# Slots turned by the expert's number, one expert's transposes queued later, and a rearranged last sequence

## The chip, the cores and the metric

The kernel runs on one core of one Trainium2 chip. The metric is the device time of one execution in microseconds (us). Before the change three runs gave 1287.1, 1283.97 and 1284.54 us; the median is 1284.54 us.

## The reference, cut to what matters

One layer of a hybrid decoder over 512 tokens of 1024 channels in float32: a mixer (an mLSTM head group beside causal pooling), then a mixture of experts, then a last RMSNorm.

```
x   = x + concat([ym, yp]) @ W_out
h   = RMSNorm(x)
logits = h @ w_router + b_router                    # 512 x 32
top_vals, top_idx = top_k(logits, 4)                # four experts a token
gates = softmax(top_vals)
for every expert e, for the tokens that chose it:
    gate = min(h @ w_gate[e] + b_gate[e], 7)        # 1024 x 1024
    up   = clip(h @ w_up[e] + b_up[e], -7, 7)       # 1024 x 1024
    y    = (gate * sigmoid(1.702 * gate) * (up + 1)) @ w_down[e] + b_down[e]
    x[token] += gates[token, e] * y
out = RMSNorm(x)
```

Each of the 32 experts has three weight matrices of 4 MB, so the experts' weights alone are 12 MB an expert and 403 MB (384 MiB) in all. With the reference's inputs an expert gets between 30 and 113 of the 2048 token choices.

## The kernel before

The mixer and the router take the first part of the span; from about 228 us on the kernel works through the experts. A table made in the program sets their order: experts 0 and 1 come first, and the last one has few tokens (30), so that only its blocks 0 and 1 are used and its blocks 2 and 3 are skipped by branches.

**Weights.** The SP queue streams all weights into a ring of slots of 2 MB each (128 partitions by 4 x 1024 floats; `load_chunks`, L114 to L147: w_gate and w_up by L141 as halves of 1 MB, w_down by L144 as whole slots). A load is issued as soon as its slot is free, that is, when TensorE has read the weights that lay there. The slots' names in the trace are wr, ym, wlo and whi.

**Slots of the tokens.** The router ranks each token choice among those of its expert (`place`). The rank divided by 32 is the block, and the rank modulo 32 is the slot (L710, `sfk`). A block is a tile of 128 partitions by 256 floats: token slot s with quarter q of its 1024 channels sits on partition 32q + s. POOL gathers the blocks from the table h2d by row indices (L931, 1 KB a row) and adds the results into the table yd (L1121; blocks 0 and 1 together as a pair with 2 KB a row, blocks 2 and 3 with 1 KB). Slots without a token have an index out of bounds and move no row. These transfers go through the queue that the page calls software_dynamic, beside SP's weights on the same 16 DMA engines.

**Start of the experts.** `xpose(e)` (L959) turns the gathered blocks by four VectorE transposes into the left operands xt. `softmax` (L1093 to L1097) makes the gates, `gates_rows(t)` (L1103 and L1106, VectorE) makes the rows of 128 tokens that `gates_product(t)` (L1114, TensorE) turns into gates by slot. The four products stand between the four quarters of expert 0's w_gate and w_up matmuls (`each`, L1001), so TensorE can't go on with the next quarter before the product's rows are there.

**The last sequence.** After the last expert but one the order of TensorE, VectorE, ACT and POOL is written out by hand: the string FIN (L39). A letter is a step, a digit a block or a group of 128 tokens. D and E are the first and second half of the last w_down matmuls of a block (L1069). Steps s, r and f are for the tokens not in the last expert, read back from yd by SP (L1177): the sum of squares (s, L1180 ACT), the scale (r, L1184 VectorE and L1185 POOL), and the scaling with the store to the output (f, L1188 VectorE and L1209 SP). Steps a, q, n, m and p are for the last expert's blocks: the add and its squares (a, L1214 VectorE, L1215 ACT), the sum over the four quarters (q, L1218 TensorE), the norm (n, L1222 VectorE, L1223 POOL), the multiplication (m, L1227 VectorE) and the scatter of the finished rows into the output (p, L1200 POOL, which writes over rows that the stores of f have written and so waits for all four of these).

Of the kernel before, what the change touches and what calls it, by code (L numbers as in the profile page):

```python
# [12 lines left out]
I32 = mybir.dt.int32  # L13
U32 = mybir.dt.uint32
AF = mybir.ActivationFunctionType
OP = mybir.AluOpType
# [4 lines left out]
S, D = 512, 1024  # L21
# [5 lines left out]
EPS = 1e-5  # L27
LIMIT = 7.0
ALPHA = 1.702
NB = 4  # L30
# [5 lines left out]
LN = 0  # L36

FIRST = 2
FIN = "D2 D3 D0 D1 s0 r0 s1 r1 f0 s2 r2 f1 s3 r3 f2 E2 E3 a2 a3 q2 q3 f3 n2 n3 m2 p2 m3 p3 E0 E1 a0 q0 a1 q1 n0 n1 m0 p0 m1 p1"  # L39
ENDM = ("PE", "DVE", "Activation", "Pool")  # L40
HA = (False, False)
DBG = {}
# [131 lines left out]
def mixer(tc, nc, ctx, g):  # L174
    pe, act, dve, gp, sp = nc.tensor, nc.scalar, nc.vector, nc.gpsimd, nc.sync
# [75 lines left out]
    n1 = tc.tile_pool(name="n1", bufs=1)  # L251
# [119 lines left out]
    for hpart in (hhi, hlo):  # L371
        for k in range(NK):
            pe.matmul(ps[:100], wg[:, k, :], hpart[:, k, :], start=(hpart is hhi and k == 0),
                      stop=(hpart is hlo and k == NK - 1))
# [4 lines left out]
    r, m = (at.tile([128, S], F32, name=n, tag="mb", bufs=2)[0:H] for n in "rm")  # L379
# [228 lines left out]
    def early():  # L608
# [5 lines left out]
    v8, ebk, sfk, gi, cnt, iota_e, iota_eb, tok4, qbig = (  # L614
        g[k] for k in ("v8", "ebk", "sfk", "gi", "cnt", "iota_e", "iota_eb", "tok4", "qbig"))
# [86 lines left out]
    def place(t):  # L702

        o = R[t]
        dve.tensor_tensor(o["oh"], o["oh"], o["rank"][:, None, :].to_broadcast([128, 4, NE]), op=OP.mult)
        rk, bi = (rp.tile([128, 4], I32, name=n, tag=n, bufs=2) for n in ("rk", "bi"))
        with nc.allow_low_precision("ranks are whole numbers under 512"):
            dve.tensor_reduce(rk, o["oh"], axis=AX.X, op=OP.add)
        dve.tensor_scalar(bi, rk, 5, None, op0=OP.arith_shift_right)
        dve.tensor_scalar(sfk[:, t, :], rk, 31, None, op0=OP.bitwise_and)  # L710
        dve.scalar_tensor_tensor(ebk[:, t, :], o["xf"], 16.0, bi, op0=OP.mult, op1=OP.add)
        o["s"] = rp.tile([128, 4, 32], F16, name="ohs", tag="ohs", bufs=2)
        o["e"] = rp.tile([128, 4, 128], F16, name="rh", tag="rh", bufs=1)
        dve.tensor_tensor(o["s"], iota_e[:, None, :].to_broadcast([128, 4, 32]),
                          sfk[:, t, :, None].to_broadcast([128, 4, 32]), op=OP.is_equal)
# [183 lines left out]
def moe(tc, nc, ctx, g):  # L899
    pe, act, dve, gp, sp = nc.tensor, nc.scalar, nc.vector, nc.gpsimd, nc.sync  # L900
    const, ident = (g[k] for k in ("const", "ident"))
    gi, gs, cnt, h2d, yd, sfk, ebk, gates_k, v8, iota_e, iota_eb = (
        g[k] for k in ("gi", "gs", "cnt", "h2d", "yd", "sfk", "ebk", "gates_k", "v8", "iota_e", "iota_eb"))
    W, load_chunks, rstd_of, nhalf, out = (g[k] for k in ("W", "load_chunks", "rstd_of", "nhalf", "out"))
# [3 lines left out]
    with tc.tile_pool(name="mo", bufs=1) as mo, tc.tile_pool(name="mop", bufs=1, space=PSUM) as pp:  # L908
# [5 lines left out]
        yb = pp.tile([128, 512], F32, name="yb")  # L914
# [37 lines left out]
        def xpose(e):  # L952
            XT[e] = []
            for b in range(NB):
                if e == 0 and b == 2:
                    for ps in gub[2:] + [dbq]:
                        dve.memset(ps, 0.0)
                t = mo.tile([128, 256], F32, name=f"xt{b}", tag=f"xt{b}", bufs=2) if b < 3 else xgt[:, 4]
                i = dve.transpose(t, xg[b])  # L959
                if b:  # L960
                    tc.keep_in_program_order(i)
                XT[e].append(t)
# [136 lines left out]
        def gates_rows(t):  # L1099

            o = mo.tile([128, 4, 32], F32, name="o32", tag="t", bufs=4)
            r = mo.tile([128, 4, 128], F32, name="r32", tag="t", bufs=4)
            dve.tensor_tensor(o, iota_e[:, None, :].to_broadcast([128, 4, 32]),  # L1103
                              sfk[:, t, :, None].to_broadcast([128, 4, 32]), op=OP.is_equal)
            for k in range(4):
                dve.tensor_scalar(r[:, k, :], iota_eb, ebk[:, t, k:k + 1], gates_k[:, t, k:k + 1],  # L1106
                                  op0=OP.is_equal, op1=OP.mult)
            ROWS[t] = o, r

        def gates_product(t):  # L1110
            o, r = ROWS[t]
            for k in range(4):
                for q in range(4):
                    pe.matmul(yb[q * 32:(q + 1) * 32, :128], o[:, k, :], r[:, k, :], start=(t == 0 and k == 0),  # L1114
                              stop=(t == NT - 1 and k == 3))
            if t == NT - 1:
                dve.tensor_copy(gs, yb[:, :128])
                pairs()
# [60 lines left out]
        def square(a, junk, sums, t):  # L1179
            act.activation(junk, a[:, t], AF.Square, accum_out=sums[:, 2 * t:2 * t + 1])  # L1180
# [6 lines left out]
        def result(a, nfb, t):  # L1187
            dve.scalar_tensor_tensor(a[:, t], a[:, t], RS[t], nfb, op0=OP.mult, op1=OP.mult)  # L1188
# [5 lines left out]
        def finish(a, nfb, yg, nfq, junk, quarters, sums):  # L1194

            e = NE - 1
            orows = out[0].rearrange("t (q n) -> (t q) n", q=4)

            def put(b):
                i = gp.indirect_dma_start(out=orows, out_offset=bass.IndirectOffsetOnAxis(  # L1200
                    ap=gi[:, e * NB + b:e * NB + b + 1], axis=0), in_=zs[b], in_offset=None,
                    bounds_check=S * 4 - 1, oob_is_err=False)
                for o in puts.values():
                    tc.declare_no_dep(i.ins, o.ins, reason="an expert's tokens differ")
                puts[b] = i

            def store(t):
                result(a, nfb, t)
                sp.dma_start(out[0, t * 128:(t + 1) * 128, :], a[:, t])  # L1209

            zs = [yg[:, b * 256:(b + 1) * 256] for b in range(NB)]

            def add(b):
                dve.scalar_tensor_tensor(zs[b], db[b], gs[:, e * NB + b:e * NB + b + 1], zs[b], op0=OP.mult, op1=OP.add)  # L1214
                act.activation(junk[:, :256], zs[b], AF.Square, accum_out=sums[:, 2 * b:2 * b + 1])  # L1215

            def sumq(b):
                pe.matmul(yb[:, b:b + 1], quarters, sums[:, 2 * b:2 * b + 1], start=True, stop=True)  # L1218

            def norm(b):  # L1220
                r = sums[:, 2 * b + 1:2 * b + 2]
                dve.tensor_scalar(r, yb[:, b:b + 1], 1.0 / D, EPS, op0=OP.mult, op1=OP.add)  # L1222
                gp.tensor_tensor(r, r, nhalf[:, 0:1], op=OP.pow)  # L1223

            def mul(b):
                r = sums[:, 2 * b + 1:2 * b + 2]
                dve.scalar_tensor_tensor(zs[b], zs[b], r, nfq, op0=OP.mult, op1=OP.mult)  # L1227

            def final_put(b):
                with tc.If(GR[e] > 32 * b) if b > 1 else ExitStack():  # L1230
                    put(b)

            todo = dict(s=lambda t: square(a, junk, sums[:, 8:], t), r=lambda t: scale(sums[:, 8:], t), f=store, a=add, q=sumq, n=norm, m=mul, p=final_put,
                        d=lambda b: some(e, d_mm, b, range(8)), D=lambda b: some(e, d_mm, b, range(4)),
                        E=lambda b: some(e, d_mm, b, range(4, 8)))
            for step in FIN.split():
                todo[step[0]](int(step[1]))
# [7 lines left out]
        xpose(0)  # L1245
        softmax()
        gates_rows(0)
        gates_rows(1)
        g["order"].close()
        order = ExitStack()  # L1250
        order.enter_context(tc.manual_schedule(engines={mybir.EngineType.PE}))
# [1 line left out]
        for kind, e in g["way"]:  # L1253
            if kind == "gu":
                with tc.issue_after(last[0]):
                    CR[e] = pe.value_load(tokens(e), min_val=0, max_val=S)
                if e + 1 < NE:
                    gather(e + 1)
                    xpose(e + 1)
                if e:  # L1260
                    bias(0, gb, 0, 512)
                    act.activation(gbs, gb, AF.Copy)
                if e + 1 < NE:
                    select(e + 1, 0)
                each(e, gu_mm)
                load_chunks(4)
                if e == NE - 1:
                    select(e, 1)
                act_blocks(e)
                continue  # L1270
            if e < NE - 1:
                select(e, 1)
                halves(e)
                each(e, d_mm)
            load_chunks(2)
            if e < NE - 1:
                scatter_all(e)
            if e == NE - 2:
                final = finish_early()
                order.close()  # L1280
                end = ctx.enter_context(ExitStack())
                end.enter_context(tc.manual_schedule(engines={getattr(mybir.EngineType, n) for n in ENDM}))
# [137 lines left out]
```

## Time and profile before

| | |
|---|---|
| median of three runs | 1284.54 us |
| the profiled execution's own time | 1286.53 us |
| its span | 1284.8 us |
| TensorE busy | 1160.3 us (90%) |
| VectorE busy | 496.6 us (39%) |
| moved by DMA | 454.54 MB, mean 354 GB/s |
| of it software_dynamic (gathers, scatters) | 17.59 MB in 11264 packets |
| granted TensorE clock, mean | 0.968 |

The span is the profiled time from the first instruction to the last; the execution's own time is 1.7 us longer. The DMA share of a stretch is the mean busy share of the core's 16 DMA engines: about 1 means that all of them are busy, and a lower value means that some or all are idle. In the rows of a timeline the bracket tells how long the engine sat idle before the instruction and what ended that.

### The profile page before, as it was taken

The numbers are of one execution on the slowest core, as the hardware profiler recorded it, in microseconds if no ns is written. First come the engines' busy times: TensorE is split into PE (matmuls) and PEld (weight loads), VectorE is DVE, ScalarE is ACT, GpSimd is POOL, SyncE is SP. The second block draws the span as 40 slices with busy tenths as digits, with TensorE's granted clock in tenths as the row PEclk, the third lists the DMA queues.
The fourth block names the chain that finished last, engine by engine and source line by source line (L and its number), as shares of the span: only waits on it lengthen the run. The fifth ranks groups of instructions, "written<-read, shape, count | busy, mean of one in ns | idle before, by whom it ended". The sixth has DMA issues, their size and how long they took to land. (4 is left out here: it accounts for less than half of the span.)

```text
span 1284.8 us, 24782 instructions
## 1 busy us (share of the span) xinstructions
PE 1160.3 (90%) x9818; PEld 497.6 (39%) x9819; DVE 496.6 (39%) x1263; ACT 274.2 (21%) x592; POOL 212.8 (17%) x259
## 2 busy tenths in 40 slices
PE   8999999789887899999989998889979999989973
PEld 5787676323232233333323333233323333334321
DVE  4684756354432422234333342333332232233433
ACT  4593453102111101012111111111101011111212
POOL 3011021102211101121111211012201111111022
PEclk9999999989998999999989999889999999999997
DMA  9731766779999999999999999999999999999972
GB/s 325 253 112 33 235 228 235 265 294 405 408 412 414 419 415 387 413 390 413 407 412 406 412 404 402 414 408 404 407 404 405 406 406 404 402 400 408 411 291 83
DMA packets 81800, 454.54 MB, mean 354 GB/s; under 512 B 12766, under 2 KB 27222, under 8 KB 40283
## 3 DMA queue, kind: packets, MB, share of 16 engines
q1 hardware_dynamic: 67674, 428.58, 82.6%
q0 software_dynamic: 11264, 17.59, 5.6%
q10 hardware_dynamic: 2688, 5.90, 1.3%
q8 instruction: 129, 2.11, 0.7%
q14 instruction: 45, 0.36, 0.1%
HBM read 439.69 MB, written 16.92 MB: 355 GB/s over the span
## 5 line engine op out<-in xcount | busy, mean ns | idle before, releaser
L1001 PE MATMUL gub<-wr,xt 128*32 128x512 f32 x3520 | 409.6, 616 | 48.2 <-PEq L979 15.3
L1011 DVE TENSOR_TENSOR t<-gub,gbs 128x512 f32<-128x512 f32 x128 | 85.4, 686 | 565.9 <-PE gub L1001 340.8
L1001 PEld LDWEIGHTS gub<-wr,xt 128*32 128x32 f32 x3520 | 131.7, 113 | 308.5 <-issue 294.8
L931 POOL DMA_INDIRECT xgt<-h2d,gi x81 | 83.5, 1031 | 728.2 <-DVE t L1012 511.4
L949 ACT ACTIVATE par<-ident 128x128 fp32r<-128x128 f32 x64 | 19.4, 305 | 448.0 <-PEq L981 214.7
L1014 ACT ACTIVATE sg<-t 128x256 f32<-128x256 f32 x128 | 52.4, 413 | 250.9 <-DVE t L1012 250.9
L1389 DVE TENSOR_TENSOR sg<-sg,t 128x256 f32<-128x256 f32 x128 | 52.4, 423 | 87.4 <-ACT sg L1014 87.2
L1055 PE MATMUL dbp<-wr,at 128*32 128x512 f32 x736 | 84.1, 604 | 0.0
L1055 PE MATMUL yb<-wr,at 128*32 128x512 f32 x672 | 76.4, 594 | 0.1
L1001 PE MATMUL gub<-whi,xt 128*32 128x512 f32 x512 | 60.4, 607 | 6.0 <-DMA whi<-in_w_up_dram 6.0
L1121 POOL DMA_INDIRECT yd<-yp,gip x31 | 50.3, 1623 | 92.0 <-ACT yp L1133 87.2
L1001 PE MATMUL gub<-wlo,xt 128*32 128x512 f32 x512 | 58.8, 594 | 6.8 <-DMA wlo<-in_w_up_dram 3.1
L1001 PE MATMUL gub<-ym,xt 128*32 128x512 f32 x512 | 61.2, 607 | 3.0 <-DMA ym<-in_w_up_dram 3.0
L1021 DVE STREAM_TRANSPOSE at<-sg 128x256 f32<-128x256 f32 x96 | 60.9, 635 | 0.1
L1390 DVE SCALAR_TENSOR_TENSOR sg<-t,sg 128x256 f32<-128x256 f32 x128 | 49.8, 409 | 0.1
L240 DVE TENSOR_TENSOR wlo<-wraw,whi 128x1024 fp32r<-128x1024 f32 x30 | 36.7, 1223 | 28.7 <-ACT whi L239 28.6
L959 DVE STREAM_TRANSPOSE xt<-xgt 128x256 f32<-128x256 f32 x96 | 40.8, 426 | 6.0 <-DMA xgt<-h2d,gi 6.0
L1055 PEld LDWEIGHTS dbp<-wr,at 128*32 128x32 f32 x736 | 23.3, 111 | 50.5 <-issue 47.5
L1069 PE MATMUL dbq<-wr,at 128*32 128x256 f32 x672 | 39.6, 384 | 0.8 <-DMA wr<-in_w_down_dram 0.8
L239 ACT ACTIVATE whi<-wraw 128x1024 fp32r<-128x1024 f32 x30 | 31.7, 1059 | 40.0 <-PE sc L294 11.0
L1055 PEld LDWEIGHTS yb<-wr,at 128*32 128x32 f32 x672 | 21.7, 110 | 45.6 <-issue 43.9
L1015 DVE TENSOR_SCALAR t<-t 128x256 f32<-128x256 f32 x128 | 36.4, 284 | 0.0
(366 smaller groups left out, 1318.1 us busy)
## 6 DMA issues: line engine op xcount, KB each, us to landing
wr<-in_w_down_dram SPq DMA_DIRECT2D x45, 2048.0 KB
wr<-in_w_gate_dram SPq DMA_DIRECT2D x89, 1024.0 KB
wr<-in_w_up_dram SPq DMA_DIRECT2D x89, 1024.0 KB
ym<-in_w_gate_dram SPq DMA_DIRECT2D x13, 1024.0 KB
ym<-in_w_up_dram SPq DMA_DIRECT2D x13, 1024.0 KB
wlo<-in_w_gate_dram SPq DMA_DIRECT2D x13, 1024.0 KB
wlo<-in_w_up_dram SPq DMA_DIRECT2D x13, 1024.0 KB
whi<-in_w_gate_dram SPq DMA_DIRECT2D x13, 1024.0 KB
```

Source lines behind the costliest of these rows:

```text
L240: low.tensor_tensor(l3, rv, h3.bitcast(F32), op=OP.subtract)
L931: return gp.indirect_dma_start(out=xg[b], out_offset=None, in_=h2d, in_offset=bass.IndirectOffsetOnAxis(ap=(gi0 if e < FIRST else gi)[:, e ...
L959: i = dve.transpose(t, xg[b])
L1001: i = pe.matmul(gub[b][q * 32:(q + 1) * 32, :], XT[e][b][:, c * 32:(c + 1) * 32], w[:, :, c % 2, q * 256:(q + 1) * 256], start=(c == 0), s ...
L1011: dve.tensor_tensor(t, gub[b], gbs, op=OP.add)
L1014: act.activation(sg, t[:, 0:256], AF.Sigmoid, scale=ALPHA)
L1021: dve.transpose(AT[e, b].rearrange("p (c s) -> p c s", c=8), sgs[b].rearrange("p (i c) -> p c i", c=8))
L1055: i = pe.matmul(dbp[r:r + 32, :], AT[e, b][:, c * 32:(c + 1) * 32], w[:, c % 4, h * 512:(h + 1) * 512], start=False, stop=(c == 7))
L1069: i = pe.matmul(quarter(e, b)[q * 32:(q + 1) * 32, :], AT[e, b][:, c * 32:(c + 1) * 32], w[:, c % 4, q * 256:(q + 1) * 256], start=False, ...
L1121: i = gp.indirect_dma_start(out=to, out_offset=bass.IndirectOffsetOnAxis(ap=index, axis=0), in_=y, in_offset=None, bounds_check=rows - 1, ...
L1389: dve.tensor_tensor(sg, sg, t[:, 0:256], op=OP.mult)
L1390: dve.scalar_tensor_tensor(sg, t[:, 256:], 1.0, sg, op0=OP.add, op1=OP.mult)
```

## The change

Three things are changed.

First, the slot of a token choice is no longer its rank modulo 32 but that number turned by exclusive-or with the number of its expert (L710, one VectorE instruction for one). The block stays the same. For an expert whose tokens fill no whole block, the rows that are missing were always those of the highest slots; now they lie elsewhere for each expert.

Second, the transposes of expert 1 may be issued on VectorE only behind the last instruction of `gates_rows(1)`.

Third, FIN is reordered: E of all blocks comes ahead of the adds, the four adds stand together ahead of f2 and f3, and one norm over the four blocks takes the place of four. The scatters of blocks 2 and 3, which are branched around here, come last.

```diff
-FIN = "D2 D3 D0 D1 s0 r0 s1 r1 f0 s2 r2 f1 s3 r3 f2 E2 E3 a2 a3 q2 q3 f3 n2 n3 m2 p2 m3 p3 E0 E1 a0 q0 a1 q1 n0 n1 m0 p0 m1 p1"
+FIN = "D2 D3 D0 D1 s0 r0 s1 r1 f0 s2 r2 f1 s3 r3 E2 E3 E0 E1 a2 a3 a0 a1 f2 q2 q3 q0 q1 f3 n0 m0 p0 m1 p1 m2 p2 m3 p3"
...
-        dve.tensor_scalar(sfk[:, t, :], rk, 31, None, op0=OP.bitwise_and)
+
+        dve.scalar_tensor_tensor(sfk[:, t, :], rk, 31, o["xf"].bitcast(I32), op0=OP.bitwise_and, op1=OP.bitwise_xor)
...
-                dve.tensor_scalar(r[:, k, :], iota_eb, ebk[:, t, k:k + 1], gates_k[:, t, k:k + 1],
-                                  op0=OP.is_equal, op1=OP.mult)
+                i = dve.tensor_scalar(r[:, k, :], iota_eb, ebk[:, t, k:k + 1], gates_k[:, t, k:k + 1],
+                                      op0=OP.is_equal, op1=OP.mult)
             ROWS[t] = o, r
+            return i
...
-            def norm(b):
-                r = sums[:, 2 * b + 1:2 * b + 2]
-                dve.tensor_scalar(r, yb[:, b:b + 1], 1.0 / D, EPS, op0=OP.mult, op1=OP.add)
-                gp.tensor_tensor(r, r, nhalf[:, 0:1], op=OP.pow)
+            rq = sums[:, NB:2 * NB]
+
+            def norm(_):
+                dve.tensor_scalar(rq, yb[:, 0:NB], 1.0 / D, EPS, op0=OP.mult, op1=OP.add)
+                gp.tensor_tensor(rq, rq, nhalf, op=OP.pow)
...
-        gates_rows(1)
+        rows_made = gates_rows(1)
...
-                    xpose(e + 1)
+                    with ExitStack() if e else tc.issue_after(rows_made.ins):
+                        xpose(e + 1)
```

Where a line number of the changed kernel is meant, it is one higher than before from L711 on, two or three higher from the end of `gates_rows` on.

VectorE at the start of the experts, before. The first row is softmax's, the four transposes (xt_2152 to xgt) are expert 1's, gip is the index table of the pairs, o and r are the rows of the gates:

```order
L1093 TENSOR_SCALAR nv<-v_68 128x4
L959 STREAM_TRANSPOSE xt_2152<-xgt 128x256
L941 UNCONDITIONAL_BRANCH
L959 STREAM_TRANSPOSE xt_2154<-xgt 128x256
L959 STREAM_TRANSPOSE xt_2156<-xgt 128x256
L959 STREAM_TRANSPOSE xgt<-xgt 128x256
L1084 TENSOR_SCALAR gip<-gi 32x32 x2
L971 UNCONDITIONAL_BRANCH
L941 UNCONDITIONAL_BRANCH
L1084 TENSOR_SCALAR gip<-gi 32x32 x2
L1096 RECIPROCAL nv<-nv 128x4
L1097 TENSOR_TENSOR gates_k<-gates_k,nv 128x16
```

Behind these rows stand the rows of gates_rows(0) and gates_rows(1).

The same place in the changed kernel:

```order
L1094 TENSOR_SCALAR nv<-v_68 128x4
L1085 TENSOR_SCALAR gip<-gi 32x32
L942 UNCONDITIONAL_BRANCH
L1085 TENSOR_SCALAR gip<-gi 32x32 x3
L1097 RECIPROCAL nv<-nv 128x4
L1098 TENSOR_TENSOR gates_k<-gates_k,nv 128x16
L1104 TENSOR_TENSOR o_2103<-iota_e,sfk 128x128
L1107 TENSOR_SCALAR r_2104<-iota_eb,ebk,gates_k 128x128 x4
L1104 TENSOR_TENSOR o_2110<-iota_e,sfk 128x128
L1107 TENSOR_SCALAR r_2111<-iota_eb,ebk,gates_k 128x128 x4
L960 STREAM_TRANSPOSE xt_2152<-xgt 128x256
L960 STREAM_TRANSPOSE xt_2154<-xgt 128x256
```

The gates and the rows of the first two products now stand ahead of expert 1's transposes; nothing else changes places with them.

VectorE in the last sequence, before, from r3 on. wr_13381 holds the token groups, wr_13382 the last expert's blocks and the sums; gub_2041, gub_2042, dbp and dbq are the matmul results of blocks 2, 3, 0 and 1:

```order
L1184 TENSOR_SCALAR wr_13382<-wr_13382 128x1
L1188 SCALAR_TENSOR_TENSOR wr_13381<-wr_13381,wr_13382 128x1024
L1214 SCALAR_TENSOR_TENSOR wr_13382<-gub_2041,gs,wr_13382 128x256
L1214 SCALAR_TENSOR_TENSOR wr_13382<-gub_2042,gs,wr_13382 128x256
L1188 SCALAR_TENSOR_TENSOR wr_13381<-wr_13381,wr_13382 128x1024
L1222 TENSOR_SCALAR wr_13382<-yb 128x1 x2
L1227 SCALAR_TENSOR_TENSOR wr_13382<-wr_13382 128x256 x2
L1214 SCALAR_TENSOR_TENSOR wr_13382<-dbp,gs,wr_13382 128x256
L1230 UNCONDITIONAL_BRANCH x2
L1214 SCALAR_TENSOR_TENSOR wr_13382<-dbq,gs,wr_13382 128x256
L1222 TENSOR_SCALAR wr_13382<-yb 128x1 x2
L1227 SCALAR_TENSOR_TENSOR wr_13382<-wr_13382 128x256 x2
```

These are f2, a2, a3, f3, then norm and multiplication of blocks 2 and 3, and last the same steps for blocks 0 and 1.

And in the changed kernel:

```order
L1186 TENSOR_SCALAR wr_13382<-wr_13382 128x1
L1216 SCALAR_TENSOR_TENSOR wr_13382<-gub_2041,gs,wr_13382 128x256
L1216 SCALAR_TENSOR_TENSOR wr_13382<-gub_2042,gs,wr_13382 128x256
L1216 SCALAR_TENSOR_TENSOR wr_13382<-dbp,gs,wr_13382 128x256
L1216 SCALAR_TENSOR_TENSOR wr_13382<-dbq,gs,wr_13382 128x256
L1190 SCALAR_TENSOR_TENSOR wr_13381<-wr_13381,wr_13382 128x1024 x2
L1225 TENSOR_SCALAR wr_13382<-yb 128x4
L1229 SCALAR_TENSOR_TENSOR wr_13382<-wr_13382 128x256 x4
```

The four adds come first, f2 and f3 behind them, and one norm instruction is left of four.

TensorE in the last sequence, before (yb are the sums over the quarters, dbp and dbq the second halves of blocks 0 and 1):

```order
L1218 MATMUL yb<-wr_13382 128x1 x2
L1069 MATMUL dbp<-wr_13091,at_13583 32x256 x16
L1069 MATMUL dbq<-wr_13091,at_13593 32x256 x5
L1230 UNCONDITIONAL_BRANCH x2
L1069 MATMUL dbq<-wr_13091,at_13593 32x256 x11
L1218 MATMUL yb<-wr_13382 128x1 x2
```

And in the changed kernel:

```order
L987 UNCONDITIONAL_BRANCH x2
L1070 MATMUL dbp<-wr_13091,at_13583 32x256 x16
L1070 MATMUL dbq<-wr_13091,at_13593 32x256 x16
L1220 MATMUL yb<-wr_13382 128x1 x4
L1232 UNCONDITIONAL_BRANCH x2
```

E0 and E1 no longer stand behind the sums of blocks 2 and 3.

## Rows read from the trace of the kernel before

**Rows 1.** The page: the span, and one DMA queue (packets, MB, share).

```profile
span 1284.8 us, 24782 instructions
...
q0 software_dynamic: 11264, 17.59, 5.6%
```

**Rows 2.** Windows: engines' busy time, then granted clock, DMA share, GB/s.

```profile
1100.00:1200.00 100.00, 93.14 (x860) 35.73 (x856) 35.70 (x96) 15.88 (x41) 16.44 (x12) 0.98 1.01 405
```

**Rows 3.** Timeline at the experts' start: start, duration, engine, line, instruction.

```profile
228.89 5.36 PE L1001 MATMUL gub<-wr,xt 128*32 128x512 f32 x48 [0.64 <-DVE xt L959]
...
229.36 0.99 POOL L931 DMA_INDIRECT xgt<-h2d,gi  x1 [0.30 <-issue]
...
231.64 0.19 ACT L1095 ACTIVATION_READ_ACCUMULATOR gates_k<-v,nv 128x1 f32 x1
...
236.33 0.45 DVE L959 STREAM_TRANSPOSE xt<-xgt 128x256 f32<-128x256 f32 x1 [5.78 <-DMA xgt<-h2d,gi]
...
238.06 0.74 DVE L1084 TENSOR_SCALAR gip<-gi 32x32 int32<-32x32 int32 x4
...
239.34 1.11 DVE L1106 TENSOR_SCALAR r<-iota_eb,ebk,gates_k 128x128 f32<-128x128 f16 x4
...
239.73 1.93 PE L1114 MATMUL yb<-r,o 128*32 128x128 f32 x32 [5.49 <-DVE o L1103]
```

**Rows 4.** Windows behind that, same columns as in group 2.

```profile
240.00:250.00 10.00, 9.54 (x124) 4.06 (x120) 3.97 (x16) 0.00 (x0) 0.00 (x0) 0.86 0.46 167
...
270.00:280.00 10.00, 10.00 (x80) 2.59 (x76) 6.00 (x17) 0.82 (x2) 0.00 (x0) 0.83 0.43 161
280.00:290.00 10.00, 9.53 (x112) 3.99 (x104) 2.02 (x5) 0.33 (x2) 1.00 (x1) 1.00 1.00 425
```

**Rows 5.** Windows at the end of the weights and of the reads of yd.

```profile
1224.00:1242.00 18.00, 16.54 (x142) 5.36 (x138) 5.69 (x14) 2.21 (x5) 2.75 (x3) 0.95 0.86 317
1242.00:1258.00 16.00, 11.20 (x112) 4.50 (x104) 5.24 (x12) 0.83 (x2) 2.10 (x2) 0.89 0.48 176
```

**Rows 6.** The chain that ended last, its longest link in the last sequence.

```profile
1242.04 17.30 DMA wr<-yd
```

**Rows 7.** Timeline of the last sequence.

```profile
1255.50 2.39 PE L1069 MATMUL dbq<-wr,at 128*32 128x256 f32 x32
...
1258.19 1.06 ACT L1180 ACTIVATE wr<-wr 128x1024 f32<-128x1024 f32 x1 [6.37 <-DMA wr<-yd]
...
1261.96 1.06 ACT L1180 ACTIVATE wr<-wr 128x1024 f32<-128x1024 f32 x1
...
1263.48 0.15 DVE L1184 TENSOR_SCALAR wr<-wr 128x1 f32<-128x1 f32 x1
...
1265.20 0.87 DVE L1214 SCALAR_TENSOR_TENSOR wr<-gub,gs,wr 128x256 f32<-128x256 f32 x2
...
1265.99 1.27 DVE L1188 SCALAR_TENSOR_TENSOR wr<-wr,wr 128x1024 f32<-128x1024 f32 x1
...
1267.42 3.25 PE L1069 MATMUL dbp<-wr,at 128*32 128x256 f32 x32
...
1270.49 1.90 PE L1069 MATMUL dbq<-wr,at 128*32 128x256 f32 x32
...
1272.47 0.48 DVE L1214 SCALAR_TENSOR_TENSOR wr<-dbq,gs,wr 128x256 f32<-128x256 f32 x1 [1.24 <-PE dbq L1069]
...
1274.27 1.06 POOL L1223 TENSOR_TENSOR wr<-wr,small 128x1 f32<-128x1 f32 x2 [5.44 <-DVE wr L1222]
...
1275.63 1.14 POOL L1200 DMA_INDIRECT out_dram<-wr,gi  x1 [0.30 <-DVE wr L1227]
1277.08 0.99 POOL L1200 DMA_INDIRECT out_dram<-wr,gi  x1 [0.31 <-DVEq L1298]
```

**Rows 8.** Windows of the last store's traffic.

```profile
1269.00:1270.00 1.00, 1.00 (x16) 0.42 (x12) 0.34 (x1) 0.00 (x0) 0.00 (x0) 0.50 0.43 164
1270.00:1271.00 1.00, 1.00 (x24) 0.61 (x20) 0.26 (x1) 0.00 (x0) 0.00 (x0) 0.93 0.00 0
```

More of the change, by code (lines that the diff above doesn't have):

```diff
@@ L1214, in add @@
                 dve.scalar_tensor_tensor(zs[b], db[b], gs[:, e * NB + b:e * NB + b + 1], zs[b], op0=OP.mult, op1=OP.add)
-                act.activation(junk[:, :256], zs[b], AF.Square, accum_out=sums[:, 2 * b:2 * b + 1])
+                act.activation(junk[:, :256], zs[b], AF.Square, accum_out=sums[:, b:b + 1])
             def sumq(b):
-                pe.matmul(yb[:, b:b + 1], quarters, sums[:, 2 * b:2 * b + 1], start=True, stop=True)
-            def norm(b):
-                r = sums[:, 2 * b + 1:2 * b + 2]
-                dve.tensor_scalar(r, yb[:, b:b + 1], 1.0 / D, EPS, op0=OP.mult, op1=OP.add)
-                gp.tensor_tensor(r, r, nhalf[:, 0:1], op=OP.pow)
+                pe.matmul(yb[:, b:b + 1], quarters, sums[:, b:b + 1], start=True, stop=True)
+            rq = sums[:, NB:2 * NB]
+            def norm(_):
+                dve.tensor_scalar(rq, yb[:, 0:NB], 1.0 / D, EPS, op0=OP.mult, op1=OP.add)
+                gp.tensor_tensor(rq, rq, nhalf, op=OP.pow)
             def mul(b):
-                r = sums[:, 2 * b + 1:2 * b + 2]
-                dve.scalar_tensor_tensor(zs[b], zs[b], r, nfq, op0=OP.mult, op1=OP.mult)
+                dve.scalar_tensor_tensor(zs[b], zs[b], rq[:, b:b + 1], nfq, op0=OP.mult, op1=OP.mult)
             def final_put(b):
```

## Prediction

> **What bounds the kernel now.** I read the page first: the span is 1284.8 us, and the gathers and scatters of the tokens (software_dynamic) take 5.6% of the 16 DMA engines' span, 0.056 x 1284.8 = 72 us of each engine [rows 1]. Then the windows. A hundred microseconds late in the experts show a DMA share of 1.01 at 405 GB/s while TensorE is busy for 93 of 100 us [rows 2]: the stream of weights through the DMA engines is what cannot go faster, and TensorE has some slack. But the stream is not full from the beginning. Between 240 and 250 us the share is 0.46, between 270 and 280 us 0.43 with TensorE busy all the time, and only from 280 us on it is 1.00 [rows 4]. Until then the ring waits for TensorE to free slots, so each microsecond that TensorE loses before 280 us is a microsecond by which the full stream starts later, and nothing behind it can win it back.
>
> At the other end the share falls again before all is there. From 1224 to 1242 us it is 0.86, and from 1242 to 1258 us it is 0.48 [rows 5], though SP asks for the reads of yd at 1242.04 and the chain waits 17.30 us for one of them [rows 6]. Four reads of 512 KB are 2.1 MB; at 405 GB/s that is 5 us. So some engines have emptied their queues and others, still full of older work, hold the reads back: the last sequence starts at 1258.19 us, with ACT 6.37 us idle for the reads [rows 7]. The timeline from there to the last scatter at 1277.08 us is a chain of small steps.
>
> The change touches all three places: the start (transposes), the uneven end of the DMA engines (slots), and the chain of small steps (FIN).
>
> **Start.** TensorE ends its first quarter of expert 0 at 228.89 + 5.36 = 234.25 us and then idles until 239.73, 5.49 us, for the rows of the first gates [rows 3]. The gates' exponentials were done at 231.83. VectorE could have gone on there, but stood at expert 1's first transpose from 230.5 to 236.33, waiting 5.78 us for the gather that POOL issued at 229.36 [rows 3]. The change puts that transpose behind the rows. Then VectorE does gip before the exponentials end (0.74 us, free of the wait), and from 231.8 on what took from 238.83 to 239.73 before, 0.9 us, to the moment when the product could start: ready at about 232.8, the second rows by 234.1, both ahead of 234.25. TensorE's wait goes as a whole: 5.5 us. What is late next? Expert 1's transposes still end near 238.06, where gip followed them [rows 3], as the gather decides; TensorE wants them only with expert 1's first matmuls, behind three more quarters of expert 0 of some 5.4 us each. The third and fourth rows wait for a product, as before. POOL's gathers of expert 2 wait for the same transposes, whose time doesn't change. The shares in [rows 4] say that the stream then fills 5.5 us earlier. Bounds: nothing less than 3 us, if the rows take until 236.7 because VectorE shares its time with expert 0's transposes; no more than 6.5, if the next products come closer too. I take **-5.5**.
>
> **Slots.** One VectorE instruction on 128x4 for one of the same size, four in all, in the router: nothing. What it does is to spread rows. I counted, from the reference's routing of its inputs, the KB of gather, pair and block rows that fall on each group of four slots: 1252, 1208, 1176, 1060, 944, 892, 824, 776 before (mean 1016.5), and 984, 980, 996, 1032, 1060, 1040, 1024, 1016 after. Suppose that a row's slot decides which DMA engine moves it, which no row here shows. Then the fullest engines carry 1252/1016.5 - 1 = 23% more than 72 us, 16.7 us too much, and after the change 4%, 3.1 us: 13.5 us less. The rows at the end bound this from the other side: the idle shares are 18 x 0.14 + 16 x 0.52 = 10.8 us of all 16 engines [rows 5]; evenly spread work would have ended that much sooner and no more. At the other end it is worth 0, if what makes some engines late is not the slots; a loss is a rival below. TensorE limits the gain too: with the new order its last matmuls would end at 1255.50 + 2.39 + 3.25 + 1.90 = 1263.04 us [rows 7], 0.6 us ahead of the scale of the last token group (1263.63). What goes beyond that must also come to TensorE as earlier weights. Between 0 and -10.8 the rows stand nearer to the upper one, since the idle share is measured; but a part of it is the gap between the last weights and the reads, which stays. I take **-8**.
>
> The Trainium skill (DMA: Bandwidth & Descriptors, "The descriptor swizzle") says that in a 128-partition transfer each engine writes a fixed set of partitions, four neighbours at a time, and that slots 0 to 3 of a quarter go to engine 0 or 8, slots 28 to 31 to engine 7 or 15. By that rule my supposition holds and the whole 13.5 us are at stake; without it the slots have nothing to do with the engines and the term is 0. The falling share at the end agrees with uneven engines, but which ones they are it does not tell.
>
> **Last sequence.** The reference point is r3, which ends at 1263.63 us and stays. Before: f2, a2, a3 and f3 to 1267.26, while E0 started at 1267.42 only behind the sums of blocks 2 and 3, E1 ended at 1272.39, a1 came at 1272.47, the last norm's power at 1274.27, p0 at 1275.63, p1 at 1277.08 [rows 7]. After: E0 and E1 follow D1 and are done at 1263.04. On VectorE the four adds take 0.87 + 2 x 0.48 = 1.83 us, to 1265.5, then f2 and f3 at 1.27 each, to 1268.0 (0.7 later than before). The norm's way from the first power to p0 was 1.36 us; with the one norm behind f3 that gives p0 at about 1269.6. But p0 also waits for the stores. The last store's traffic was still there in the slice from 1269 to 1270 (share 0.43) and gone in the next [rows 8], 2.2 to 2.7 us behind f3's end at 1267.26. So the last store lands near 1270.7 after, and p0 waits for that: the wait changes from TensorE's matmuls to the store. p1 follows 1.45 us later, at 1272.2 to 1272.4, 4.7 us sooner. The branches of p2 and p3 now come behind p1; with idle times of 0.3 us around each put [rows 7] I charge 0.5. Sum **-4.2**; bounds -2.5 (the store's landing takes 2 us longer) and -6 (p0 goes at 1269.6). Three VectorE and three POOL instructions less are inside of this.
>
> **Sum.** -5.5 - 8 - 4.2 = -17.7 us. The profiled execution took 1286.53 us, 1.7 above its span and 2.0 above the median; by it 1268.8, on the median 1284.54 it is **1266.8 us**.
>
> **Rivals.**
>
> (a) The slots do nothing for the end, because the late engines are late for another reason. For: no row ties a slot to an engine. Against: the row counts are steep, and 16.7 us is of the size of the 17.30 us wait. Start and last sequence alone: 1284.54 - 9.7 = 1274.8.
>
> (b) The late engines vanish wholly, with 10.8 to 13.5 us in place of 8: 1261 to 1264. For: the even counts after. Against: TensorE's end, only 0.6 us behind.
>
> (c) The wait at the start comes back a little later, for instance at expert 1's first matmuls, so that only about 0 to 2 of the 5.5 us stay: 1284.54 - 12.2 - 1 = 1271.3. For: the stream's share of 0.43 at 270 us shows a second place where TensorE's slots were awaited. Against: TensorE was busy all of these 10 us [rows 4].
>
> (d) Slower: the late engines are those of the high slots. These have been spared until now, with 776 of 1016.5 KB; the change gives them 1016. That is 24% of 72 us, 17 us more on the engines that already end last. The sum is -9.7 + 17 = +7.3: 1291.8. It decides against the change when the reads of yd come more than 9.7 us later than 1258.19. For: the end shows late engines but not their slots. Against: they would have to be much slower than the others, as they had 38% fewer rows than the fullest.
>
> The Trainium skill (DMA: Bandwidth & Descriptors, "Latency and other measured facts") says that engines 7 and 15 are usually slower than the others in traces, and these are the engines of slots 28 to 31 in its swizzle; that is the rule that speaks for (d). This trace shows no engine by number, and the time by it is that of (d).
>
> (e) The change doesn't reach the end: what is saved is eaten by engines that end as late as before, within 0.3%: about 1284.
>
> **How the numbers follow.** Chances: my forecast 0.45, (a) 0.25, (b) 0.12, (c) 0.08, (d) 0.05, (e) 0.05. A measurement of this kernel tells 0.3%, 3.9 us, from no change. Forecast, (a), (b) and (c) are all faster by more than that: 0.90. Same 0.05, slower 0.05. The range takes in the lower bounds (-6 - 13.5 - 6 = -25.5, 1259) and (a) with weak bounds (-3 - 2.5 = -5.5, 1279): 1258 to 1279.
>
> **What would show it.** Start: the first gates product near 234.3 with no wait for VectorE, the transposes of expert 1 behind the rows, a DMA share of 1 from about 275 us on. Slots: from the last weights to the last reads of yd a share that stays high and then falls at once; ACT's first square within about 8 us of SP's reads and not 16; the gathers and scatters with the same packets and MB. Last sequence: E0 right behind D1, four adds in a row, one norm on 128x4, and p0 at most 3 us behind f3. Measured from r3, p1 should start about 8.7 us later, not 13.5. Wrong would be: a wait of TensorE at expert 1's xt, a square that still starts 16 us behind SP's reads (then (a)), or later than that (then (d)).

## The result and the profile after

The changed kernel took 1268.43 us (median of four runs, 1268.07 to 1268.54) against 1285.37 us for the kernel before (four runs, 1283.97 to 1287.1). The ratio is 0.9865, with a 95% interval of 0.9852 to 0.9878: some 17 us less. The profiled execution took 1268.07 us with a span of 1266.4 us. The forecast was 1266.8 us, within 1258 to 1279.

The timeline at the start of the experts, to be set beside [rows 3] (line numbers are one or two higher now):

```profile
228.53 5.36 PE L1002 MATMUL gub<-wr,xt 128*32 128x512 f32 x48 [0.67 <-DVE xt L960]
...
234.33 1.08 PE L1116 MATMUL yb<-r,o 128*32 128x128 f32 x32 [0.45 <-DVE r L1107]
235.23 5.33 PE L1002 MATMUL gub<-wr,xt 128*32 128x512 f32 x48
...
231.57 0.18 DVE L1097 RECIPROCAL nv<-nv 128x4 f32<-128x4 f32 x1 [0.61 <-ACT gates_k L1096]
...
235.44 0.45 DVE L960 STREAM_TRANSPOSE xt<-xgt 128x256 f32<-128x256 f32 x1 [1.02 <-DMA xgt<-h2d,gi]
```

TensorE goes on to the first product at 234.33 us in place of 239.73. It idles 0.45 us ahead of it, not 5.49. The transposes of expert 1 still wait for their gather, but TensorE doesn't wait for them (POOL's next gather does: POOL is idle for 6.21 us ahead of it, before for 6.72). The product takes 1.08 us where it took 1.93. The windows of the kernel before tell why; the column behind the five busy times is the granted clock:

```profile
234.30:239.70 5.40, 0.00 (x0) 0.00 (x0) 2.99 (x13) 0.00 (x0) 2.00 (x2) 0.96 1.00 369
239.70:242.50 2.80, 2.77 (x40) 1.90 (x44) 2.74 (x12) 0.00 (x0) 0.00 (x0) 0.50 0.98 407
242.50:247.00 4.50, 4.50 (x47) 1.08 (x36) 0.55 (x3) 0.00 (x0) 0.00 (x0) 0.97 0.15 56
```

Behind its idle time TensorE worked at half clock (0.50, the 1.2 GHz level) for about 3 us: the 2.8 us of the second window, and a small part of the third, whose mean is 0.97. In the changed kernel, which doesn't idle there, it is 1.00 from 234 to 247 us:

```profile
234.00:240.00 6.00, 5.67 (x80) 2.33 (x80) 3.16 (x11) 0.00 (x0) 2.00 (x2) 1.00 1.00 384
240.00:247.00 7.00, 6.54 (x88) 2.33 (x80) 1.32 (x5) 0.00 (x0) 0.00 (x0) 1.00 1.01 390
```

The end of the reads of yd, to be set beside [rows 5]: SP asked for them at 1225.53 us and the first square started at 1239.28.

```profile
1208.00:1226.00 18.00, 16.83 (x146) 5.46 (x138) 5.61 (x14) 2.21 (x5) 1.67 (x1) 0.99 0.90 342
1226.00:1239.00 13.00, 8.51 (x104) 3.60 (x100) 5.22 (x12) 0.83 (x2) 2.09 (x2) 1.00 0.76 289
```

The DMA share there is 0.76 in place of 0.48, and the stretch is 3 us shorter. The last sequence, to be set beside [rows 7]:

```profile
1239.28 1.06 ACT L1182 ACTIVATE wr<-wr 128x1024 f32<-128x1024 f32 x1 [4.35 <-DMA wr<-yd]
...
1244.58 0.15 DVE L1186 TENSOR_SCALAR wr<-wr 128x1 f32<-128x1 f32 x1
1244.64 0.87 DVE L1216 SCALAR_TENSOR_TENSOR wr<-gub,gs,wr 128x256 f32<-128x256 f32 x2
...
1246.21 2.47 DVE L1190 SCALAR_TENSOR_TENSOR wr<-wr,wr 128x1024 f32<-128x1024 f32 x2
...
1248.60 0.15 DVE L1225 TENSOR_SCALAR wr<-yb 128x4 f32<-128x4 f32 x1
1248.83 1.02 POOL L1226 TENSOR_TENSOR wr<-wr,small 128x4 f32<-128x4 f32 x1 [3.25 <-DVE wr L1225]
...
1254.56 1.06 POOL L1202 DMA_INDIRECT out_dram<-wr,gi  x1 [4.71 <-SPq L1301]
1255.92 0.98 POOL L1202 DMA_INDIRECT out_dram<-wr,gi  x1 [0.30 <-issue]
```

r3 started 18.90 us earlier than before (1263.48 to 1244.58). The first scatter p0 starts 9.83 us behind r3's end, where it was 12.00: 2.2 us won. But the span ends 11.8 us behind p0's start, where it was 9.1: 2.7 us lost. The rows of the skipped branches of blocks 2 and 3 show it, first of the kernel before, then of the changed one (columns: number, shortest, median and longest in ns, first and last start):

```profile
L1230 POOLq INC_SWDGE_SEM  x2: 1107/1113/1119, 1268.0 to 1269.3; - x2
```

```profile
L1232 POOLq INC_SWDGE_SEM  x2: 1142/1150/1157, 1255.0 to 1256.4; - x2
```

Each of these branches is not taken and still puts one instruction of 1.1 us on POOL's queue; by its name it counts up the semaphore of the scatter that is left out. Before, the two ran at 1268 us, while POOL had to wait for the last sums anyway. Now they run behind the start of p0, and the end of the program comes later by what they take.

### The profile page after: what moved, and what is told of

It is laid out like the page before. It is cut to its first block, busy times and chain, and to the rows that moved or that the text cites. A ratio compares the mean times of both kernels' runs of the same rounds, so it can differ in the third digit from the quotient of the medians.

```text
span 1266.4 us, 24772 instructions
## 1 busy us (share of the span) xinstructions
PE 1151.1 (91%) x9818; PEld 496.1 (39%) x9819; DVE 496.1 (39%) x1260; ACT 274.4 (22%) x592; POOL 211.5 (17%) x256
## 3 DMA queue, kind: packets, MB, share of 16 engines
q0 software_dynamic: 11264, 17.59, 5.7%
q8 instruction: 129, 2.11, 0.7%
## 5 line engine op out<-in xcount | busy, mean ns | idle before, releaser
L1002 PE MATMUL gub<-wr,xt 128*32 128x512 f32 x3520 | 403.2, 609 | 42.2 <-DMA wr<-in_w_down_dram 8.4
```

What stands on the lines that cost most here:

```text
L1002: i = pe.matmul(gub[b][q * 32:(q + 1) * 32, :], XT[e][b][:, c * 32:(c + 1) * 32], w[:, :, c % 2, q * 256:(q + 1) * 256], start=(c == 0), s ...
```

## The experiments

All ratios are to the kernel before, on the same chip. The runs came in three series of four kernels; the kernel before had medians of 1285.61, 1285.1 and 1285.81 us in them.

**One part at a time.** The slots alone:

```diff
-        dve.tensor_scalar(sfk[:, t, :], rk, 31, None, op0=OP.bitwise_and)
+        dve.scalar_tensor_tensor(sfk[:, t, :], rk, 31, o["xf"].bitcast(I32), op0=OP.bitwise_and, op1=OP.bitwise_xor)
```

> The kernel before with the slots turned by the expert's number and nothing else. Theory (read from the two traces: r3 came 18.9 us earlier, of which the start explains some 7.2): the slots give -11.7 us, to a ratio of 0.991. The prediction's own term: -8, ratio 0.994. Rival, that the late engines have nothing to do with the slots: 0, ratio 1.000. By the theory the DMA share between SP's reads of yd and the first square stays higher than before (0.48).

Measured: 1275.74 us, ratio 0.9931 (0.9917 to 0.9945), so -8.9 us (-7.1 to -10.7). The rival of no effect is out; between -8 and -11.7 it lies nearer to the prediction's term. The wait behind SP's reads shrank as it should:

```profile
1236.41 1.75 SPq L1177 DMA_DIRECT2D wr<-yd  x4
...
1246.45 1.06 ACT L1180 ACTIVATE wr<-wr 128x1024 f32<-128x1024 f32 x1 [4.36 <-DMA wr<-yd]
```

From SP's request to the first square it is 10.0 us; before it was 16.5 (1241.66 to 1258.19).

The transposes alone:

```diff
-                    xpose(e + 1)
+                    with ExitStack() if e else tc.issue_after(rows_made.ins):
+                        xpose(e + 1)
```

> The kernel before with expert 1's transposes behind the gates' rows and nothing else. Theory: -7.3 us (ratio 0.9943), since TensorE wins back not only the wait of 5.5 us but also the slower product and quarter behind it (1.93 in place of 1.08 us, 5.96 in place of 5.33). The prediction's term: -5.5 (0.9957). Rival, that the wait only moves to expert 1: about -1 (0.999). By the theory the DMA queues are full about 7 us sooner and stay so.

Measured: 1278.8 us, 0.9948 (0.9935 to 0.9961), so -6.7 us (-5.0 to -8.4). The interval holds both -5.5 and -7.3; the trace speaks for the longer one. SP's loads run ahead by 7.2 us in it, and the end waits as long as before:

```profile
274.38 0.34 SPq L141 DMA_DIRECT2D wr<-in_w_gate_dram  x1
...
1233.74 1.76 SPq L1178 DMA_DIRECT2D wr<-yd  x4
...
1250.07 1.06 ACT L1181 ACTIVATE wr<-wr 128x1024 f32<-128x1024 f32 x1 [6.01 <-DMA wr<-yd]
```

The first of these loads in the kernel before:

```profile
281.55 0.34 SPq L141 DMA_DIRECT2D wr<-in_w_gate_dram  x1
```

It is 7.2 us sooner: 0.4 by which the whole stretch came sooner, 5.5 of the wait less the 0.45 that is left, 0.85 of the product and 0.63 of the quarter behind it (5.33 for 5.96 us), the rest within what the reading leaves open. Without the 0.4, which is not the change's, that is 6.8 us. The rival of a wait that only moves is out.

SP asks for the same loads in the same order in all these runs, so the time at which it asks for one of them tells how far a run is ahead there. One load in the middle, first in the kernel before, then with the slots alone, then with the transposes alone:

```profile
826.78 0.33 SPq L141 DMA_DIRECT2D wlo<-in_w_up_dram  x1
```

```profile
821.54 0.33 SPq L141 DMA_DIRECT2D wlo<-in_w_up_dram  x1
```

```profile
819.50 0.33 SPq L141 DMA_DIRECT2D wlo<-in_w_up_dram  x1
```

| us ahead of the kernel before | load at 281.55 | at 826.78 | at 1049.41 | first square, 1258.19 |
|---|---|---|---|---|
| slots alone | 0.6 | 5.2 | 6.9 | 11.7 |
| transposes alone | 7.2 | 7.3 | 7.3 | 8.1 |

The lead of the transposes is there from the start and stays. The lead of the slots grows along the whole stream: 6.9 of its 11.7 us are there at 1049 us, long before the end. (These two executions of the slots alone and of the kernel before are 11.1 us apart, more than the 8.9 of the ratio.)

The last sequence alone (the new FIN and the one norm):

```diff
-FIN = "... s3 r3 f2 E2 E3 a2 a3 q2 q3 f3 n2 n3 m2 p2 m3 p3 E0 E1 a0 q0 a1 q1 n0 n1 m0 p0 m1 p1"
+FIN = "... s3 r3 E2 E3 E0 E1 a2 a3 a0 a1 f2 q2 q3 q0 q1 f3 n0 m0 p0 m1 p1 m2 p2 m3 p3"
```

> The kernel before with the new order of the last steps and the one norm, and nothing else. Theory: about 0 (-1.5 to +1.5 us, ratio 0.999 to 1.001): the first scatter comes some 2 to 4 us sooner after r3, but the skipped branches of blocks 2 and 3, now behind the scatters, cost POOL 2.7 us between the first scatter and its last drain (6.84 us in place of 4.14). The prediction's term: -4.2 (0.9967). Rival: slower by 3, when the last store lands as late after f3 as in the changed kernel (5.0 us in place of some 3).

Measured: 1285.33 us, 0.9999 (0.9990 to 1.0008), so 0 (-1.3 to +1.0). The -4.2 of the prediction is out. p0 waits for the stores here too:

```profile
1266.20 2.47 DVE L1190 SCALAR_TENSOR_TENSOR wr<-wr,wr 128x1024 f32<-128x1024 f32 x2
...
1274.36 1.06 POOL L1202 DMA_INDIRECT out_dram<-wr,gi  x1 [4.52 <-SPq L1300]
```

f3 ends at 1268.67, p0 starts 5.7 us later. The three ratios multiply to 0.9878; the changed kernel measured 0.9865 and, in a second series, 0.9871. The parts add up within their intervals.

**Both without the last sequence.** The slots and the transposes, with FIN and the norms as before:

> The changed kernel with the last steps and the four norms as before, so the slots and the transposes alone. Theory (read from the run with the slots alone, where the last scatter starts 14.2 us behind r3, and 11.3 in the changed kernel, less the 2.7 us of the two branches): the same as the changed kernel, 1268.4 to 1269. The prediction's term: 4.2 us slower, 1272.6.

Measured: 1269.68 us, 0.9880 (0.9864 to 0.9897). The changed kernel itself, on the same chip:

> The changed kernel itself, once more, so that the next three can be compared with it on one chip: 1268.4 us, ratio 0.9865 to 0.9870.

Measured: 1268.34 us, 0.9871 (0.9852 to 0.9890). So the last sequence is worth 1.3 us there by the medians, with intervals that overlap for the most part. These two runs alone tell neither 0 nor 4.2 us with certainty; the run with the last sequence alone excludes 4.2.

**Is it the load by slots?** The mirror of the old slots, in the changed kernel:

```diff
-        dve.scalar_tensor_tensor(sfk[:, t, :], rk, 31, o["xf"].bitcast(I32), op0=OP.bitwise_and, op1=OP.bitwise_xor)
+        dve.tensor_scalar(sfk[:, t, :], rk, 31, 31, op0=OP.bitwise_and, op1=OP.bitwise_xor)
```

> The changed kernel with the slots turned by exclusive-or with 31 for all experts, in place of the expert's number: slot 0 becomes 31, so the KB by group of four slots are those of before in mirror order, 776 to 1252. Theory (a row's slot decides which engine moves it, and the fullest engines end last): the gain of the slots is lost again, 1268.4 + 11.7 = 1280, a ratio to the kernel before of 0.996. Rival (d) of the prediction, that the engines of the high slots are slower by themselves: at least 5 us more than that, 1285 or above (1.000). Rival, that slots don't matter: 1268 (0.987).

Measured: 1277.66 us, 0.9944 (0.9931 to 0.9957). That is 9.2 us above the changed kernel's 1268.43 (on another chip), and the same as the transposes alone (0.9948): the gain of the slots is gone. The high slots' engines are not slower by themselves, since the kernel with the full load on the high slots is no slower than the one with it on the low slots. Rival (d) of the prediction is out, and the rule of the Trainium skill that spoke for it (DMA: Bandwidth & Descriptors, "Latency and other measured facts": engines 7 and 15 are usually slower) decides nothing here.

Slots turned by half:

```diff
-        dve.scalar_tensor_tensor(sfk[:, t, :], rk, 31, o["xf"].bitcast(I32), op0=OP.bitwise_and, op1=OP.bitwise_xor)
+        dve.tensor_scalar(sfk[:, t, :], rk, 31, None, op0=OP.bitwise_and)
+        dve.scalar_tensor_tensor(sfk[:, t, :], o["xf"].bitcast(I32), 16, sfk[:, t, :], op0=OP.bitwise_and, op1=OP.bitwise_xor)
```

> The changed kernel with the slots turned by exclusive-or with 16 for the upper sixteen experts alone, in place of each expert's number. The KB by group of four slots are then 1068, 1028, 980, 916, 1128, 1072, 1020, 920: the fullest stands 11.0% above the mean, where it was 23.2% without any turning and is 4.3% by the expert's number. Theory (the fullest group sets the end): 65% of the slots' gain of some 9 us, so 3.2 us slower than the changed kernel: 1271.6. Rival, that any mixing of the slots evens the engines: the same as the changed kernel, 1268.4.

Measured: 1274.67 us, 0.9921 (0.9907 to 0.9935), 6.3 us above the changed kernel. It stands between the two as the loads do, so not any mixing will do; but it keeps a third of the gain and not two thirds. The fullest group alone is too simple a rule. Its fullest group is the fifth (1128 KB), and the engines that are late in it may have other work on top; which is not settled.

Rows of one half of the partitions left out, but for the gathers of the first two experts. The first kernel leaves out those of partitions 0 to 63, its twin those of 64 to 127:

```diff
-    dve.tensor_scalar(gi, pl_[:, 128:256], qbig, None, op0=OP.add)
+    dve.tensor_scalar(gi[64:128], pl_[64:128, 128:256], qbig[64:128], None, op0=OP.add)
+    dve.tensor_scalar(gi[0:64], pl_[0:64, 128:256], 3.0 * BIG, None, op0=OP.add)
```

> The changed kernel with the row indices of the gathers and scatters out of bounds on partitions 0 to 63 (but for the gathers of experts 0 and 1). It leaves out those partitions' rows, half of every expert's channels. If a row's partition decides its DMA engine, eight of the 16 engines lose nearly all of their 72 us of rows. Theory (from the packet records of the changed kernel: instruction fetches fall on one half of the engines, and it is this half that ends late): one of this run and its twin gains 8 to 20 us (the other half then sets the end), the other gains less than 3 us. Rival, that any engine serves any row: both gain alike, by half of some 70 us as far as the DMA bounds, 15 to 30 us. Rival, that the late engines are no half: both gain less than 3 us.

> The twin: the row indices out of bounds on partitions 64 to 127. It leaves out these rows. Theory and rivals as for its twin: one of the two gains 8 to 20 us and the other less than 3, or both alike 15 to 30, or both less than 3.

Measured: 1269.61 us (0.9886, 0.9869 to 0.9902) without the low half's rows and 1268.23 us (0.9872, 0.9856 to 0.9889) without the high half's. Neither gains, though in each the software_dynamic queue moved 9.41 MB in place of 17.59. Had any engine served any row, both should have gained, by the estimate above 15 to 30 us. So rows stay with engines; the late ones lie in both halves, and my theory of one late half falls. The trace's landing events say the same. Each weight load signals 16 times; for a load at about 1200 us (1150 to 1165 us in the last two) these signals fell as follows, the distance taken from the middle of the earlier ones:

| kernel | early | late, and by how much |
|---|---|---|
| before | 13 | 3, by 8 to 18 us |
| transposes alone | 13 | 3, by 9 to 18 us |
| slots alone | 8 | 8, by 11 to 16 us |
| mirror | 11 | 5, by 8 to 18 us |
| half turned | 9 | 7, by 9 to 18 us |
| changed | 8 | 8, by 12 to 18 us |
| changed, low half's rows left out | 10 | 6, by 10 to 16 us |
| changed, high half's rows left out | 14 | 2, by 14 us |

Six engines stay late when the low half's rows are gone, and two when the high half's are: together the eight. My reading is that three engines held the stream back in the kernel before, and that eight share this now. Why eight of them are still 12 us and more behind the others stays open. No run here tries what else may load them, for instance the instruction fetches (q8 on the page: 129 packets, 2.11 MB).

**The last sequence mended.** The two branches ahead of the scatters:

```diff
-... q0 q1 f3 n0 m0 p0 m1 p1 m2 p2 m3 p3"
+... q0 q1 f3 n0 m2 p2 m3 p3 m0 p0 m1 p1"
```

> The changed kernel with the steps m2 p2 m3 p3 ahead of m0 p0 m1 p1, so that POOL takes the two skipped branches while it waits for the last store. Theory: POOL's 6.84 us from the first scatter to its last drain go back to about 4.1, -2.7 us to the changed kernel's 1268.4: 1265.7, a ratio to the kernel before of 0.9845. Rival, that the branches themselves wait for the stores or end later than the store lands: p0 comes 2.7 us later and nothing is won, 1268.4 (0.9865).

> The changed kernel with m2 p2 m3 p3 ahead of m0 p0 m1 p1 again, now on one chip with the changed kernel. Theory: -2.7 us to it, as POOL's time from the first scatter to its last drain was 2.7 us shorter in the first run's profile. Rival: 0, as the first run's median (0.4 us less, on another chip) seemed to say.

Measured: 1268.02 us (0.9871, 0.9854 to 0.9887), and in the second series, beside the changed kernel's 1268.34, 1266.87 us (0.9855, 0.9840 to 0.9870). In the second one's trace the branches run while POOL waits for the store, and p0 starts 9.85 us behind r3's end, as late as without them:

```profile
L1232 POOLq INC_SWDGE_SEM  x2: 1107/1113/1119, 1248.4 to 1249.7; - x2
```

```profile
1253.99 1.06 POOL L1202 DMA_INDIRECT out_dram<-wr,gi  x1 [4.73 <-SPq L1301]
```

From p0 to the end of the span (1263.1) it is 9.1 us in place of 11.8. In the trace the 2.7 us are back; in the medians it is 0.4 and 1.5 us, within the runs' scatter. It has the lowest median of all, but a gain over the changed kernel is not shown by the times. The traces show it more clearly, since the time from r3's end to the end of the span leaves out where r3 came: 18.7 and 19.0 us in these two runs, 21.4 to 21.7 us in the seven with the branches behind p1 (the stores earlier, below, not counted), and 21.1 to 21.8 us in the four with the old sequence. So the new last sequence as it stands won nothing there, and with the branches ahead of the scatters some 2.5 us.

The stores earlier, with f2 and f3 ahead of the adds (`s3 r3 f2 f3 E2 E3 E0 E1 a2 a3 a0 a1 q2 ...`):

> The changed kernel with f2 and f3 ahead of the four adds. Theory: the last store is asked for 1.4 us sooner and lands that much sooner, the first scatter then waits for the norm, whose adds come 2.5 us later, and starts at 8 us after r3 in place of 10: -1.5 to -2 us, 1266.6 (0.9855). Rival, that what delays the last store is an instruction fetch on its DMA engine and no matter of when it is asked for: 0, 1268.4. Rival, that VectorE's order was right and the norm is late now: +0.5 or more.

Measured: 1268.28 us, 0.9874 (0.9857 to 0.9890). The step itself goes as the theory had it:

```profile
1246.93 2.48 DVE L1190 SCALAR_TENSOR_TENSOR wr<-wr,wr 128x1024 f32<-128x1024 f32 x2 [0.38 <-POOL wr L1187]
...
1252.73 0.16 DVE L1225 TENSOR_SCALAR wr<-yb 128x4 f32<-128x4 f32 x1 [1.75 <-PE yb L1220]
...
1254.81 1.06 POOL L1202 DMA_INDIRECT out_dram<-wr,gi  x1 [0.82 <-DVE wr L1229]
```

p0 now waits for the norm and starts 8.25 us behind r3's end (1246.56), 1.6 less than in the changed kernel. But r3 came 1.8 us later in this execution, more than that gain, so the time can't tell. From r3's end to the end of the span it is 20.1 us, some 1.5 less than in the changed kernel, in this one trace.

## Why the prediction was right, and where it was not

**The whole.** -17.7 us forecast, -17 measured. Two terms were a little small and one was wrong. That the sum came within 1 us is luck in part: the errors cancelled. (The range's lower sum takes 6 us for the start, where its own bound is 6.5, and 13.5 for the slots, where its own bound is 10.8; the measured time is inside either way.)

**Start, -5.5 forecast, -6.7 measured.** The mechanism was right: VectorE's wait for a gather of expert 1 held up TensorE, and the stream's gap before 280 us kept all of it. The size missed the clock: TensorE, having idled 5.5 us, worked the next 3 us or so at half clock. The rows for it stood in the trace (product 1.93 us against 1.08 for the three later ones). The bound of 6.5 us for "the next products come closer" was the right thought, priced a little low.

**Slots, -8 forecast, -8.9 measured alone.** The mechanism, that row load stays with engines by slot and that the fullest engines hold the others back, is supported by the mirror (gain gone), the half turn (in between) and the two halves left out (no gain from either). The place was wrong: I priced the term by the idle share at the end, 10.8 us "and no more", but some 7 of the 11.7 us of lead are there by 1049 us, while the stream is still full. That the size came out near is luck to that extent. The row counts add up to 8.1 MB, about half of what the queue moved; only their proportion enters. What the load doesn't explain is the eight late engines that remain. Rival (a), no effect of the slots, and rival (d), slow engines of the high slots, are refuted.

**Last sequence, -4.2 forecast, 0 measured (-1.3 to +1.0).** This step failed, in two of its terms. I had the last store land 2.2 to 2.7 us behind f3's end, and p0 start at once; p0 started 5.9 us behind f3's end (1248.68 to 1254.56). A window of the changed kernel shows most of the store through by 1251 and a remainder trickling:

```profile
1249.00:1251.00 2.00, 0.00 (x0) 0.00 (x0) 1.12 (x3) 0.00 (x0) 0.85 (x1) 0.50 0.97 375
1251.00:1254.00 3.00, 0.00 (x0) 0.00 (x0) 0.55 (x2) 0.00 (x0) 0.00 (x0) 0.50 0.09 29
```

And of the queues in these last 3 us (packets, MB, share of 16 engines):

```profile
q1 hardware_dynamic: 17, 0.05, 4.6%
q8 instruction: 1, 0.02, 2.4%
q14 instruction: 3, 0.02, 2.3%
```

Instruction fetches run in the same 3 us as the last 17 packets of the store. The traces of all runs tell more. A store, too, signals 16 times as it lands. The last of these signals came 3.0 us behind the store's issue in the four kernels with the old sequence (in the kernel before at 1270.28, 3.0 us behind f3's end, so I had read it 0.3 to 0.8 us too early). In the nine kernels with the new sequence and f3 behind the adds it came after 4.7 to 5.0 us. In each of these nine one 16 KB instruction fetch (q8, 1.0 to 1.5 us) runs during the store, and a packet of the store starts within 0.02 us of the fetch's end, with about ten more one by one behind it. With f2 and f3 ahead of the adds no such fetch falls there, and the last signal came after 3.1 us. Here are 2 us from 1.3 us behind the issue on, first in the changed kernel, then with the stores earlier:

```profile
q1 hardware_dynamic: 102, 0.36, 46.6%
q8 instruction: 1, 0.02, 3.3%
q14 instruction: 1, 0.01, 1.0%
```

```profile
q1 hardware_dynamic: 105, 0.36, 46.8%
q14 instruction: 1, 0.01, 1.0%
```

So one of the store's shares waits behind an instruction fetch; why the fetch falls just there was not tried. From the last signal to p0 it is another 0.9 us (1253.69 to 1254.56), which I had put at nothing. With the store that late, p0 gained 2.2 us and not 4.9. The second term is the two branches of p2 and p3, charged with 0.5 us and in truth 2.7 (from p0 to the end of the span it is 9.1 us in all six traces with the branches ahead, 11.8 in all eight with them behind): I took them for idle times of 0.3 us, though each puts a POOL instruction of 1.1 us on the queue, which could be read at 1268 us in the trace of before.

**What would have shown it.** The first product at 234.3 came at 234.33; the full stream came at 270 to 280 us (share 0.98 against 0.43); the first square came 13.75 us behind SP's reads in the changed kernel's profile and 9.3 in that of its second series, with 8 forecast; p1 came 11.2 us behind r3's end in place of 8.7.

## What to carry to other kernels

Before the stream that bounded this kernel was full, each microsecond of TensorE's wait counted in full, and a bit more because TensorE came back at half clock. When transfers share engines with a bounding stream, count bytes by partition group and not in sum, over the whole stream and not at its end alone: spreading short rows evenly over the slots was worth 8.9 us of 1285 at no cost in instructions. And when steps are moved behind the last long wait, count every queue entry that they leave behind, skipped branches included.

## What the runs showed of the hardware

- A skipped branch around a scatter put one semaphore instruction on POOL's queue, 1.11 to 1.16 us each; two of them behind the last scatters cost 2.7 us.
- TensorE's granted clock was 0.50 in the 2.8 us behind an idle time of 5.5 us, and 0.97 in the 4.5 us behind that.
- An instruction fetch of 16 KB (1.0 to 1.5 us) during the last store went with a landing 4.7 to 5.0 us behind the issue in nine traces; without one there it was 3.0 to 3.1 us in five.
- Leaving out the gathered and scattered rows of one half of the partitions (9.41 MB left of 17.59) brought no gain (0.9886 and 0.9872 against 0.9865 to 0.9871); six and two engines stayed late in its landing signals.
